# Turning two groups of sample outputs by VectorE and DMAs, later head sums, gates a head ahead, another last norm

## The chip, the cores and the metric

One core of a Trainium2 chip. The metric is the device time of one launch, in microseconds (us). The kernel before takes 2647.93 us, the median of 3 runs (2647.58 to 2648.16).

## What is computed

One inference step of a decoder with two layers on 320 tokens: a prompt of 256 new tokens and 8 samples of 8 new tokens each, width 2048, float32. Layer 0 mixes tokens by gated linear attention (GLA, 4 heads, with a carried state for each sample), layer 1 by a chunked spatial gate (SG); each layer has a squared-ReLU MLP of width 8192 behind it, and every block ends in a layer norm. The parts that the change touches, cut from the reference:

```python
def gla_chunked(q, k, v, log_a, s0):
    ...
        scores = jnp.where(causal, jnp.einsum('bhtk,bhsk->bhts', q_dec, k_inv), 0.0)
        o = (jnp.einsum('bhtk,bhkv->bhtv', q_dec, s)
             + jnp.einsum('bhts,bhsv->bhtv', scores, vi))
        s_new = (jnp.exp(b_last[..., 0, :])[..., None] * s
                 + jnp.einsum('bhsk,bhsv->bhkv', k_to_end, vi))
        return s_new, o

def gla_mixer(x, w_in, w_gate, b_gate, norm_g, w_out, s0):
    ...
    o, s_fin = gla_chunked(q, k, v, log_a, s0)
    o = o * lax.rsqrt(jnp.mean(jnp.square(o), axis=-1, keepdims=True) + HEAD_NORM_EPS) * norm_g
    o = o.reshape(bsz, t, GLA_VAL_DIM).astype(x.dtype) * jax.nn.silu(r)
    return o @ w_out, s_fin.astype(s0.dtype)

def layer_norm(x, g, b):
    ...
    return ((xf - mu) * lax.rsqrt(var + LN_EPS) * g + b).astype(x.dtype)
```

## The kernel before

**Weights and products.** Activations stand transposed: 128 features on the partitions, 320 tokens along the free axis (prompt 0 to 255, samples 256 to 319). Every weight matrix streams once from memory in units of 512 KB (128 x 1024 values). SyncE starts the load into `raw`; ScalarE casts it to fp32r, `wh` (L176); VectorE subtracts for the rest, `wl` (L177). A unit feeds 24 matmuls of 128x128 by 128x320, three for each product (`mm3`, L194 to L196: low weight by high activation, high by low, high by high). Four units are kept in a ring, so ScalarE can be at most four units ahead of TensorE. I call these matmuls "products" and count them from the start of GLA: w_in takes 96 units, products 1 to 2304; w_out begins with product 2305.

**GLA, head by head.** Each of four heads has 24 units of w_in: 8 for v (`project_v`), 8 for k and q (`project_kq`), 8 for r (`project_r`). Between units, a `Side` runs a step of a list. `Head.steps` is the list that starts with `project_r` of its head and goes on through the next head's `project_v`: scores (`sample_scores`, `prompt_scores`), outputs of the prompt (`prompt_o`), of the first sample group (`sample_first`, `sample_group`), splits of carried states into three bf16 parts (`split`), the new prompt state (`prompt_state`, which needs `split_kv`, the high and low parts `vk` of v and k), the second sample group, then `sums` (squares summed over the head's features and rsqrt, `rs`), `weigh` (gate and norm weight) and `finish` (times `rs`). For the last head the list has only the 8 units of `project_r` and 2 more.

A sample group's output comes out of TensorE with tokens on partitions and must be turned. `sample_out` copies it out of PSUM (`os`), has TensorE transpose it four times (L688), and copies and adds the three bf16 parts. `turn_out` instead turns 32x32 blocks on VectorE, adds the parts, and lets 16 small DMAs of GpSimd's queue put the blocks in place; `place_out` copies the result into `o_all`. Before, heads 0 to 2 use `turn_out` for one group and `sample_out` for the other; head 3 uses `sample_out` for both.

**w_out** starts with units whose activations are split ahead: `split_early` makes `early` (feature blocks 0 to 2) in storage that `vk` and others used, and `split_rest` makes `oh` and `ol` for the rest, head 3's last.

**The order.** A scheduler decides the order on each engine when the program is built, from the order of the code, buffers and dependences; on the chip an engine runs its list in that order. PSUM tiles `gl` (the small products), `vfm` (one buffer, used by `turn_out`, `sums` and the decayed keys) and others are handed out in the order of the code, so a step that stands later in the code waits for the tiles of those before it.

**The last norm.** `take` gathers sums and sums of squares of the 16 feature blocks (`A_`, `Q_`), TensorE adds over partitions with matrices of ones; the last two blocks' parts go in as float32 matmuls (L882, L883). Then 14 blocks are normed as TensorE (d plus the negated mean, split high and low, by an identity matrix), VectorE (`t`, L1267) and ScalarE (`z`, L1268), and two on GpSimd (L1258 to L1260); the outputs leave by SyncE's queue (L1270, L1272).

## Time and profile before

| what | before |
| --- | --- |
| median of 3 runs | 2647.93 us |
| the profiled execution | 2648.76 us |
| its span, first to last instruction | 2647.0 us |
| mean granted TensorE clock | 0.999 |
| MB moved by DMA | 525.61 (mean 199 GB/s) |

The 1.76 us between the execution's time and its span lie outside of what the profile sees. Engines: PE is TensorE, PEld its weight loads, DVE VectorE, ACT ScalarE, POOL GpSimd, SP SyncE. A row of a timeline has the start and the busy time, both in us, engine, line, operation, output and inputs, shapes, count, and in brackets the idle time before it and what ended that. Busy times of neighbours overlap a little, so the pitch from start to start says what one costs in a row. In the groups, the numbers behind the bar are busy us, mean ns of one, and idle time before.

### The profile page before, as it was taken

To read this page: it belongs to the slowest core of one execution; us is meant where nothing else is said; L and a number is where in the kernel's file an instruction comes from. 1 tells how busy PE (TensorE), PEld (TensorE's weight loads), DVE (VectorE), ACT (ScalarE), POOL (GpSimd) and SP (SyncE) were. 2 spreads that over 40 slices of the span, in tenths; PEclk is the share of its full clock that TensorE was granted. 3 is DMA by queue.
4 is the path that set the end of the run, shared out by engine and by line. 5 is a ranking of instruction groups with operands and counts; after the bars stand their busy time and mean duration, and the time that the engine had idled before them with its cause. 6 is when DMAs were issued, how large, how long until landed. Compare 5 with 4: busy or idle time off the path is not lost.

```text
span 2647.0 us, 47028 instructions
## 1 busy us (share of the span) xinstructions
PE 2638.0 (100%) x18347; PEld 2622.7 (99%) x18347; DVE 1898.2 (72%) x2799; ACT 1335.2 (50%) x2296; POOL 438.4 (17%) x743
## 2 busy tenths in 40 slices
PE   9999999999999999999999999999999999999998
PEld 9999999999999999999999999999999999999998
DVE  7787777886666667667578797787667667766656
ACT  6666665564454445444346544465445435444434
POOL 4354320001111111111000074001111111111000
PEclk9999999999999999999999999999999999999999
DMA  8667656457676767676545456447776767776642
GB/s 257 204 178 224 207 155 232 152 179 228 216 229 217 233 215 229 214 231 207 160 152 163 154 165 196 151 138 218 219 229 216 232 214 230 215 229 215 197 153 91
DMA packets 172799, 525.61 MB, mean 199 GB/s; under 512 B 34784, under 2 KB 43744, under 8 KB 172576
## 3 DMA queue, kind: packets, MB, share of 16 engines
q1 hardware_dynamic: 129504, 409.00, 49.0%
q0 software_dynamic: 42528, 112.94, 14.2%
q8 instruction: 144, 2.36, 0.4%
q14 instruction: 79, 0.65, 0.1%
q10 hardware_dynamic: 544, 0.66, 0.1%
HBM read 493.73 MB, written 22.55 MB: 195 GB/s over the span
## 4 chain that ended last, share of the span: by engine, by line
PE 99%; ACT 0%; DMA 0%; DVE 0%; issue 0%; ACTq 0%; DVEq 0%
PE mm L194 33%; PE mm L196 32%; PE mm L195 32%; PE gl L677 0%; PE gl L629 0%; PE gl L1195 0%; PE gl L611 0%; ACT z L1268 0%; PE gl L612 0%; PE gl L590 0%; DMA raw<-gla_w_in 0%; PE gl L596 0%; PE gl L348 0%; PE gl L347 0%; PE gl L688 0%; PE gl L667 0%
## 5 line engine op out<-in xcount | busy, mean ns | idle before, releaser
L177 DVE TENSOR_TENSOR wl<-raw,wh 128x1024 fp32r<-128x1024 f32 (+1 forms) x740 | 908.3, 1229 | 638.3 <-ACT wh L176 632.1
L176 ACT CAST wh<-raw 128x1024 fp32r<-128x1024 f32 (+1 forms) x740 | 771.6, 1044 | 1054.0 <-PE mm L196 924.7
L196 PE MATMUL mm<-yh,wh 128*128 128x320 f32 x2624 | 805.4, 307 | 0.0
L194 PE MATMUL mm<-yh,wl 128*128 128x320 f32 x2624 | 802.6, 308 | 0.0
L195 PE MATMUL mm<-yl,wh 128*128 128x320 f32 x2624 | 794.1, 303 | 0.0
L194 PE MATMUL mm<-hh,wl 128*128 128x320 f32 x2048 | 630.9, 308 | 0.0
L196 PE MATMUL mm<-hh,wh 128*128 128x320 f32 x2048 | 628.8, 307 | 0.0
L195 PE MATMUL mm<-hl,wh 128*128 128x320 f32 x2048 | 619.7, 303 | 0.0
L195 PEld LDWEIGHTS mm<-yl,wh 128*128 128x128 f32 x2624 | 492.6, 188 | 0.0
L194 PEld LDWEIGHTS mm<-yh,wl 128*128 128x128 f32 x2624 | 491.1, 188 | 0.0
L196 PEld LDWEIGHTS mm<-yh,wh 128*128 128x128 f32 x2624 | 490.8, 187 | 0.0
L194 PEld LDWEIGHTS mm<-hh,wl 128*128 128x128 f32 x2048 | 384.5, 188 | 0.0
L195 PEld LDWEIGHTS mm<-hl,wh 128*128 128x128 f32 x2048 | 384.5, 188 | 0.0
L196 PEld LDWEIGHTS mm<-hh,wh 128*128 128x128 f32 x2048 | 383.0, 187 | 0.0
L990 DVE SCALAR_TENSOR_TENSOR su<-vr,pace,su 128x512 f32<-128x512 f32 x512 | 362.9, 745 | 0.0
L961 POOL DMA_DIRECT2D vr<-v_dram x256 | 138.8, 542 | 1292.2 <-DVE su L990 1280.7
L194 PE MATMUL mm<-xh,wl 128*128 128x320 f32 x768 | 237.7, 311 | 0.3 <-DVE wl L177 0.3
L196 PE MATMUL mm<-xh,wh 128*128 128x320 f32 x768 | 237.1, 309 | 0.0
L195 PE MATMUL mm<-xl,wh 128*128 128x320 f32 x768 | 234.4, 305 | 0.0
L195 PEld LDWEIGHTS mm<-xl,wh 128*128 128x128 f32 x768 | 145.0, 189 | 2.0 <-issue 1.7
L194 PEld LDWEIGHTS mm<-xh,wl 128*128 128x128 f32 x768 | 144.8, 189 | 1.7 <-issue 0.8
L196 PEld LDWEIGHTS mm<-xh,wh 128*128 128x128 f32 x768 | 144.4, 188 | 1.3 <-issue 1.3
(294 smaller groups left out, 2542.8 us busy)
## 6 DMA issues: line engine op xcount, KB each, us to landing
raw<-mlp_w SPq DMA_DIRECT2D x512, 512.0 KB, 4.0
vr<-v_dram POOLq DMA_DIRECT2D x256, 256.0 KB, 4.2
raw<-gla_w_in SPq DMA_DIRECT2D x94, 512.0 KB, 4.1
raw<-sg_w_in SPq DMA_DIRECT2D x64, 512.0 KB, 3.6
st<-state SPq DMA_DIRECT2D x32, 512.0 KB, 5.0
raw<-gla_w_out SPq DMA_DIRECT2D x32, 512.0 KB, 4.4
su<-state POOLq DMA_DIRECT2D x32, 512.0 KB, 6.4
o_state_s<-su POOLq DMA_DIRECT2D x32, 512.0 KB, 4.1
```

Of the source, the lines that this page charges most:

```text
L176: nc.scalar.copy(hi[:, ks, :], raw[:, ks, :])
L177: nc.vector.tensor_sub(lo[:, ks, :], raw[:, ks, :], hi[:, ks, :].bitcast(F32))
L194: nc.tensor.matmul(ps, wl[:, kk, s], x_h, start=first, stop=False)
L195: nc.tensor.matmul(ps, wh[:, kk, s], x_l, start=False, stop=False)
L196: nc.tensor.matmul(ps, wh[:, kk, s], x_h, start=False, stop=last)
L961: nc.gpsimd.dma_start(vt[:, 0:4, :], v_dram[h, b * DS + t].rearrange("(a f) -> a f", f=P).partition_broadcast(P))
L990: nc.vector.scalar_tensor_tensor(st[:, kt, :], v, k[:, kt : kt + 1], st[:, kt, :], op0=ALU.mult, op1=ALU.add)
```

## The change

- `WARM`: ten warming matmuls of ones at the start where there were nine.
- Heads 0 to 2 turn both sample groups by `turn_out`; `place_out` is called twice. `sample_out` with its TensorE transposes is left to head 3.
- `sums`, `weigh` and `finish` of heads 0 to 2 move behind the next head's `begin_states` and first two splits.
- The gates of heads 1 to 3 (`gate_logits`, `gate_sums`, `gate_decays`) are made in the steps of the head before.
- `prompt_scores` is ordered behind `sample_scores` on TensorE.
- The last head's `finish` and `weigh` stay in their order.
- Last norm: `A_` and `Q_` take one block more, before their ones matmuls, which now take all in float32 (`stop=True` in `total` for the other norms). The mean goes in by one matmul with a matrix `two_r` whose rows 0 and 32 are ones and the rest zeros (row 32 of `nh` holds the low part) instead of two with the identity. GpSimd has three blocks (4, 9, 13) instead of two, with two operations each instead of three; they get d plus the mean from TensorE, which ScalarE copies out of PSUM. The first four outputs leave singly.

```diff
 NU = KT // UK
-WARM = 9
+WARM = 10
 LINE = 64
...
                     d0 = c * CH if c < 2 else W0 + (c - 2) * CH
-                    nc.tensor.matmul(pc[rows, d0 : d0 + CH], hd.kip[:, kt, c * CH : (c + 1) * CH],
+                    m = nc.tensor.matmul(pc[rows, d0 : d0 + CH], hd.kip[:, kt, c * CH : (c + 1) * CH],
                                      hd.qd[:, kt, c * CH : (c + 1) * CH], start=(kt == 0 and c < 2),
                                      stop=(kt == 1 and c == NCH - 1))
+                    behind(m, hd.scored)
                     if c < NCH - 1:
...
                 ki = hd.kis[:, kt].rearrange("p b c t -> p (b c t)")
-                nc.tensor.matmul(pc[:], ki, hd.qd[:, kt, TP:T], start=(kt == 0), stop=(kt == 1))
+                hd.scored = nc.tensor.matmul(pc[:], ki, hd.qd[:, kt, TP:T], start=(kt == 0), stop=(kt == 1))
             nc.vector.copy_predicated(scs[:], mask_s[:].rearrange("p a b -> p (a b)"), pc[:])
...
         def place_out(hd):
-            o_s = o_all[:, 4 * hd.h : 4 * hd.h + 4, TP : TP + 4 * DS].rearrange("p v (j t) -> p v j t", t=DS)
+            c0 = TP + 4 * DS * (hd.g - 1)
+            o_s = o_all[:, 4 * hd.h : 4 * hd.h + 4, c0 : c0 + 4 * DS].rearrange("p v (j t) -> p v j t", t=DS)
             nc.scalar.copy(o_s, hd.got.rearrange("p j v t -> p v j t"))
...
             last = hd.h == H - 1
+            n = None if last else hds[hd.h + 1]
+            gate = (lambda: None,) * 3 if last else (n.gate_logits, n.gate_sums, n.gate_decays)
             yield lambda: None
...
             yield split(5, lambda: (last and hd.sample_out(), hd.gather_k(3)))
-            yield split(6)
-            yield split(7, lambda: last or hd.turn_out())
-            yield hd.split_kv
+            yield split(6, gate[0])
+            yield split(7, lambda: (last or hd.turn_out(), gate[1]()))
+            yield lambda: (hd.split_kv(), gate[2]())
             yield lambda: (hd.prompt_state(0), hd.prompt_state(1), hd.sample_first(), hd.sample_group())
-            yield (lambda: (hd.place_out(), hd.sample_out())) if not last else lambda: (split_early(hd), hd.sample_out())
-            yield hd.sums
-            yield hd.weigh if hd.h < H - 1 else hd.finish
-            yield hd.finish if hd.h < H - 1 else hd.weigh
-            if hd.h < H - 1:
-                n = hds[hd.h + 1]
+            if last:
+                yield lambda: (split_early(hd), hd.sample_out())
+                yield hd.sums
+                yield hd.finish
+                yield hd.weigh
+            else:
+                yield lambda: (hd.place_out(), hd.turn_out())
                 yield n.begin_states
...
                 yield lambda: n.split(1)
+                yield lambda: (hd.place_out(), hd.sums())
+                yield hd.weigh
+                yield hd.finish
...
     for h, hd in enumerate(hds):
-        gates = [hd.gate_logits, hd.gate_sums, hd.gate_decays]
         states = [lambda n=n: hd.split(n) for n in range(4)]
...
             side = Side([lambda: None, lambda: load_x(1), lambda: None, lambda: load_x(2), lambda: load_gates(),
-                         lambda: load_x(3), low_gate, *gates], 4 * NU)
+                         lambda: load_x(3), low_gate, hd.gate_logits, hd.gate_sums, hd.gate_decays], 4 * NU)
             hd.project_v(side)
...
             hd.project_v(side)
-            hd.project_kq(Side([*gates, *states[2:]], 2 * NU))
+            hd.project_kq(Side(states[2:], 2 * NU))
         side = Side(hd.steps(), 2 * NU + (2 * NU if h < H - 1 else 2))
...
             nc.tensor.matmul(p[:], ones_r[:], lo[:], start=True, stop=False)
-            nc.tensor.matmul(p[:], ones_r[:], hi[:], start=False, stop=not self.last)
+            nc.tensor.matmul(p[:], ones_r[:], hi[:], start=False, stop=True)
             return p
...
                 nc.scalar.activation(Q_, d, AF.Square)
-            elif j < KT - 2 or not self.last:
+            elif j < KT - 1 or not self.last:
                 nc.vector.tensor_add(A_, A_, d)
                 nc.vector.tensor_add(Q_, Q_, s[:])
-            if j == KT - (3 if self.last else 1):
+            if j == KT - 1 and not self.last:
                 self.pA, self.pQ = self.total(A_), self.total(Q_)
-            if j >= KT - 2 and self.last:
-                nc.tensor.matmul(self.pA[:], ones[:], d, start=False, stop=(j == KT - 1))
-                nc.tensor.matmul(self.pQ[:], ones[:], s[:], start=False, stop=(j == KT - 1))
+            elif j == KT - 1:
+                self.pA, self.pQ = gltile(T), gltile(T)
+                for p, a, b in ((self.pA, A_, d), (self.pQ, Q_, s[:])):
+                    nc.tensor.matmul(p[:], ones[:], a, start=True, stop=False)
+                    nc.tensor.matmul(p[:], ones[:], b, start=False, stop=True)
             if self.raw is not None:
...
                 nc.scalar.activation(gh, d, AF.Identity, scale=g)
-                nc.vector.scalar_tensor_tensor(gl_, d, g, gh.bitcast(F32), op0=ALU.mult, op1=ALU.subtract)
+                i = nc.vector.scalar_tensor_tensor(gl_, d, g, gh.bitcast(F32), op0=ALU.mult, op1=ALU.subtract)
+                if self.last and j == KT - 2:
+                    self.rest = i
...
             else:
-                nc.vector.tensor_add(zj, zj, ps[:])
+                i = nc.vector.tensor_add(zj, zj, ps[:])
+                if last and j == KT - 1:
+                    behind(norm.rest, i)
             norm.add(j)
...
-    on_pool = (5, 9)
+    on_pool = (4, 9, 13)
     dh, dl = norm.raw
     ps = {}
-    t_pool = l2.tile([P, T], F32, tag="s", name="t_pool")
     ident_r = l2.tile([P, P], F32R, tag="s", name="ident_r")
...
-    on_pe = [j for j in range(KT) if j not in on_pool]
+    def add_mean(j):
+        nc.tensor.matmul(ps[j][:], two_r[:], nh[:], start=False, stop=True)
+
+    on_pe = [*on_pool, *(j for j in range(KT) if j not in on_pool)]
     nh = l2.tile([P, T], F32R, tag="r", name="nh")
-    nl = l2.tile([P, T], F32R, tag="f", name="nl")
+    two_r = l2.tile([P, P], F32R, tag="vt", name="two_r")
+    nc.gpsimd.memset(two_r[:].bitcast(F32), 0.0)
+    for r in (0, 32):
+        nc.gpsimd.memset(two_r[r : r + 1].bitcast(F32), 1.0)
...
         nc.scalar.copy(nh[:], norm.nd[:])
-        nc.vector.tensor_sub(nl[:], norm.nd[:], nh[:].bitcast(F32))
+        nc.vector.tensor_sub(nh[32:33], norm.nd[32:33], nh[32:33].bitcast(F32))
...
     oT = A["o_yT"].rearrange("(k p) t -> p k t", p=P)
-    m_pool = l2.tile([P, T], F32, tag="vt", name="m_pool")
-    nc.gpsimd.tensor_mul(m_pool[:], norm.nd[:], norm.rstd[:])
+    for j in on_pool:
+        add_mean(j)
+        nc.scalar.copy(z[:, j, :], ps[j][:])
+    scaled = None
     for j in range(KT):
...
         if j in on_pool:
-            nc.gpsimd.tensor_mul(t_pool[:], y, norm.rstd[:])
-            nc.gpsimd.tensor_add(t_pool[:], t_pool[:], m_pool[:])
-            nc.gpsimd.tensor_scalar(y, t_pool[:], g, b, op0=ALU.mult, op1=ALU.add)
+            i = nc.gpsimd.tensor_mul(y, y, norm.rstd[:])
+            if scaled is not None:
+                behind(i, scaled)
+            scaled = nc.gpsimd.tensor_scalar(y, y, g, b, op0=ALU.mult, op1=ALU.add)
         else:
...
             t = l2.tile([P, T], F32, tag="t", name=nm("t"), bufs=3)
-            nc.tensor.matmul(ps[j][:], ident_r[:], nl[:], start=False, stop=False)
-            nc.tensor.matmul(ps[j][:], ident_r[:], nh[:], start=False, stop=True)
+            add_mean(j)
             nc.vector.scalar_tensor_tensor(t[:], ps[j][:], g, norm.rstd[:], op0=ALU.mult, op1=ALU.mult)
             nc.scalar.activation(y, t[:], AF.Identity, bias=b)
-        if j < 2:
+        if j < 4:
             nc.sync.dma_start(oT[:, j, :], z[:, j, :])
```

Where it moves instructions, at the places of which the prediction speaks. The rows are those of an engine's list, in order; names are tiles of the program (`mm` products, `gl` small PSUM tiles, `sp` split states, with a number that tells instances apart).

TensorE before, around head 3's `prompt_state` (L629): weight products of w_in stand ahead of it, and 48 of them behind.

```order
L194 MATMUL mm_4610<-xh_95,wl_4648 128x320
L195 MATMUL mm_4610<-xl_96,wh_4647 128x320
L196 MATMUL mm_4610<-xh_95,wh_4647 128x320
L629 MATMUL gl_4677<-vk_4641,ktp_3969 128x512 x2
L629 MATMUL gl_4677<-va_3970,vk_4641 128x512 x2
L629 MATMUL gl_4677<-vk_4641 128x512 x2
L629 MATMUL gl_4685<-vk_4641,ktp_3969 128x512 x2
L629 MATMUL gl_4685<-va_3970,vk_4641 128x512 x2
L629 MATMUL gl_4685<-vk_4641 128x512 x2
L667 MATMUL gl_4694<-va_3970,scst 128x512
```

TensorE in the changed kernel, from the end of the first sample group of head 3 (L678; the last products of w_in stand ahead of all its rows) to `prompt_state` (now L630):

```order
L678 MATMUL gl_4515<-sp_4187,qm 32x512
L689 MATMUL gl_4588<-ident,os_4586 128x128 x4
L630 MATMUL gl_4717<-vk_4681,ktp_4051 128x512 x2
L630 MATMUL gl_4717<-va_4052,vk_4681 128x512 x2
L630 MATMUL gl_4717<-vk_4681 128x512 x2
L630 MATMUL gl_4725<-vk_4681,ktp_4051 128x512 x2
L630 MATMUL gl_4725<-va_4052,vk_4681 128x512 x2
L630 MATMUL gl_4725<-vk_4681 128x512 x2
L668 MATMUL gl_4734<-va_4052,scst 128x512
```

`prompt_state` moved from behind product 2256 to behind product 2304, the last of w_in, and the transposes of `os` (L689) stand directly ahead of it.

TensorE in the changed kernel, a little later: a row of the second sample group (L678) ahead of the first products of w_out, whose activations are `early` (before, these stood directly behind the last products of w_in):

```order
L678 MATMUL gl_4734<-sp_4605,qm 32x512
L194 MATMUL mm_4862<-early_4790,wl_4870 128x320
L194 MATMUL mm_4863<-early_4790,wl_4870 128x320
L194 MATMUL mm_4864<-early_4790,wl_4904 128x320
L194 MATMUL mm_4865<-early_4790,wl_4904 128x320
L195 MATMUL mm_4862<-early_4790,wh_4869 128x320
L196 MATMUL mm_4862<-early_4790,wh_4869 128x320
```

So no product stands between the end of w_in and that place.

ScalarE before, from the cast for `vk` (L404) to the copy `os` (L685); `sr`, the gate of the last products of w_in, comes 22 rows later:

```order
L404 CAST vk_4641<-va_3970 128x1024
L613 COPY o_all_97<-gl_4456 128x2x256
L615 ACTIVATE sq_4462<-gl_4456 128x512
L406 CAST vk_4641<-ktp_3969 128x512
L613 COPY o_all_97<-gl_4465 128x2x256
L615 ACTIVATE sq_4471<-gl_4465 128x512
L657 CAST sp_4509<-st_3964 128x1024
L657 CAST sp_4560<-st_4205 128x1024
L657 CAST sp_4565<-st_4242 128x1024
L685 COPY os_4546<-gl_4475 128x512
```

ScalarE in the changed kernel, from `sr`, which reads the products up to 2304, to the copy `os` (now L686):

```order
L564 ACTIVATE sr_4858<-mm_4650 128x320
L774 CAST oh_4860<-o_all_97 128x320 x5
L176 CAST wh_4975<-raw_4974 128x1024
L774 CAST oh_4860<-o_all_97 128x320 x7
L406 CAST vk_4681<-ktp_4051 128x512
L404 CAST vk_4681<-va_4052 128x1024
L614 COPY o_all_97<-gl_4505 128x2x256
L616 ACTIVATE sq_4511<-gl_4505 128x512
L658 CAST sp_4549<-st_3929 128x1024
L658 CAST sp_4600<-st_4155 128x1024
L658 CAST sp_4605<-st_4192 128x1024
L686 COPY os_4586<-gl_4515 128x512
```

The casts for `vk`, the prompt's outputs (L614, L616), the state casts (L658) and `os` moved from before the last `sr` to behind it and behind the casts `oh` of w_out.

## Prediction

> **What bounds the kernel now.** I read the page first: its busy times, its chain, its costliest groups.
>
> ```profile
> PE 2638.0 (100%) x18347; PEld 2622.7 (99%) x18347; DVE 1898.2 (72%) x2799; ACT 1335.2 (50%) x2296; POOL 438.4 (17%) x743
> PE 99%; ACT 0%; DMA 0%; DVE 0%; issue 0%; ACTq 0%; DVEq 0%
> L176 ACT CAST wh<-raw 128x1024 fp32r<-128x1024 f32 (+1 forms) x740 | 771.6, 1044 | 1054.0 <-PE mm L196 924.7
> ```
>
> TensorE (PE) works 2638.0 of 2647.0 us and makes up 99% of the chain; ScalarE (ACT), which splits the weights, stands 924.7 us waiting for PE to give a weight buffer back. Then the waits of PE, all there are:
>
> ```profile
> PE gl L185 <- DVE ones L143: 1.1, 1, 1.1
> PE mm L194 <- DVE wl L177: 0.3, 1, 0.3
> ```
>
> PE waits 1.4 us in the whole program, both times in the first 6 us. So an edit counts only if it changes PE's work, the ends of the span, or if it makes PE wait where it does not now. Saved time on ACT, VectorE (DVE) and GpSimd (POOL) is worth nothing by itself.
>
> All sums below are against the profiled execution (2648.76 us, span 2647.0). The median shown is 0.83 lower, and I take that off at the end.
>
> **The warming matmuls, the transposes, the gates.** The start of PE's timeline (start, busy):
>
> ```profile
> 1.12 4.21 PE L185 MATMUL gl<-ones 128*128 128x128 f32 x18 [1.12 <-DVE ones L143]
> 5.59 0.87 PE L194 MATMUL mm<-xh,wl 128*128 128x320 f32 x2 [0.27 <-DVE wl L177]
> 10.00 0.47 PE L196 MATMUL mm<-xh,wh 128*128 128x320 f32 x1
> 10.27 0.42 PE L194 MATMUL mm<-xh,wl 128*128 128x320 f32 x1
> 12.71 0.31 PE L196 MATMUL mm<-xh,wh 128*128 128x320 f32 x1
> 12.85 0.31 PE L194 MATMUL mm<-xh,wl 128*128 128x320 f32 x1
> ```
>
> Nine warming matmuls are 18 records in 4.21 us; a tenth is 0.47 us more and falls mostly into the 0.27 us in which PE waits for `wl`. Bounds: +0.2 (it pushes the first product) and -1.7 (matmuls start every 0.27 us until 10.27 and every 0.14 after 12.7, so half rate ending 3.4 us sooner would give 1.7). I take 0, as the gap of 0.27 is the nearest row.
>
> Heads 0 to 2 lose the four PE transposes of the second sample group (12 in all). One set in the chain:
>
> ```profile
> 121.73 0.44 PE gl L688 x4
> ```
>
> Three sets: **-1.3 us**. What replaces them (stream transposes and adds on DVE, 48 more DMAs issued by POOL, three more table loads on ACT) runs beside the weight products of the next head, with four weight units of 24 matmuls x 0.145 = 3.5 us prepared ahead. POOL, busy 17%, has room. I cost it at nothing; were that cover gone, each microsecond beyond some 14 would show.
>
> **The last norm.** Its tail:
>
> ```profile
> 2631.80 0.48 DVE L1247 TENSOR_TENSOR nl<-nd,nh 128x320 fp32r<-128x320 f32 x1
> 2633.85 6.51 DVE L1267 SCALAR_TENSOR_TENSOR t<-mm,vec,rstd 128x320 f32<-128x320 f32 x14
> 2634.43 6.52 ACT L1268 ACTIVATE z<-t,vec 128x320 f32<-128x320 f32 x14 [2.29 <-DVE t L1267]
> 2634.71 0.87 POOL L1258 TENSOR_TENSOR t_pool<-z,rstd 128x320 f32<-128x320 f32 x1
> 2636.65 0.61 POOL L1260 TENSOR_SCALAR z<-t_pool,vec 128x320 f32<-128x320 f32 x1
> ```
>
> One of 14 steps goes to POOL: 6.51 / 14 = -0.47 us on the DVE-ACT chain. Four matmuls of the sums go ahead of it: 4 x 0.145 = -0.58. The three PSUM copies that POOL now needs (about 0.45 each, as `z`) fit into ACT's 2.29 us of idle time. POOL does 3 x (0.87 + 0.61) = 4.4 us plus gaps from 2633.9, and ends near 2638.8, before the last `z` at 2640.9. **-1.05 us**; bounds 0 (POOL or the copies late) and -1.5.
>
> **The end of head 3: a new wait.** Here work moves, and nothing is saved. The sums of head 2 now stand behind head 3's `begin_states` and first splits; PSUM tiles `gl` are handed out in that order, so head 3's scores stand behind those sums. Counted over the PE rows of both orders: head 3's scores stood behind weight product 2136 and stand now behind 2255; `prompt_state` (L629, now L630) stood behind 2256 and now behind all 2304 products of w_in. The product that starts w_out needs `early`, whose storage is that of `kqx`/`vk`, free only after L630; it is PE's next product and cannot be passed. So from T0, the end of product 2304, PE has only head 3's own small work, and that hangs on ACT. ACT's order after T0 (its rows are shown with the change): `sr` (it waits for product 2304), 12 `oh`, one `wh`, L406, L404, L614, L616, three L658, then L686 `os`. On `os` waits L689, and behind L689 on PE stand L630, L668, L678 and all of w_out. The same instructions before:
>
> ```profile
> 365.55 1.04 ACT L404 CAST vk<-va 128x1024 fp32r<-128x1024 f32 x1
> 369.15 0.62 ACT L406 CAST vk<-ktp 128x512 fp32r<-128x512 f32 x1 [1.30 <-DMA ktp<-blk]
> 369.68 0.58 ACT L613 COPY o_all<-gl 128x512 f32<-128x512 f32 x1
> 370.15 0.60 ACT L615 ACTIVATE sq<-gl 128x512 f32<-128x512 f32 x1
> 370.64 2.94 ACT L657 CAST sp<-st 128x1024 bf16<-128x1024 f32 x3
> 373.48 0.59 ACT L685 COPY os<-gl 128x512 f32<-128x512 f32 x1
> 373.95 1.06 ACT L176 CAST wh<-raw 128x1024 fp32r<-128x1024 f32 x1
> 395.95 0.44 ACT L564 ACTIVATE sr<-mm 128x320 f32<-128x320 f32 x1 [0.66 <-PE mm L196]
> 396.29 1.53 ACT L766 CAST oh<-o_all 128x320 fp32r<-128x320 f32 x4
> ```
>
> They ran in the order that the program lists, so I add starts to starts: sr 0.34, 12 oh x 0.36 = 4.3, wh 0.95, L406 0.53, L404 0.95, L614 0.47, L616 0.49, three L658 2.84, os 0.6: **`os` is there at T0 + 11.5**. PE's side and the last links:
>
> ```profile
> 369.38 1.48 PE L677 MATMUL gl<-sp,qm 128*32 128x512 bf16 x24
> 383.20 0.62 PE L629 MATMUL gl<-vk,ktp 128*128 128x512 f32 x2
> 385.98 0.40 PE L667 MATMUL gl<-va,scst 128*128 128x512 f32 x1
> 386.31 1.04 PE L677 MATMUL gl<-sp,qm 128*32 128x512 bf16 x14
> 371.79 3.49 DVE L658 TENSOR_TENSOR st<-st,sp 128x1024 f32<-128x1024 f32 x3
> 382.09 1.22 DVE L658 TENSOR_TENSOR st<-st,sp 128x1024 f32<-128x1024 f32 x1
> 384.88 1.22 DVE L660 TENSOR_TENSOR sp<-st,sp 128x1024 bf16<-128x1024 f32 x1
> 385.24 0.58 ACT L631 COPY S<-gl 128x512 f32<-128x512 f32 x1
> 386.67 0.82 ACT L766 CAST early<-o_all 128x320 fp32r<-128x320 f32 x2
> 387.16 0.89 DVE L767 TENSOR_TENSOR early<-o_all,early 128x320 fp32r<-128x320 f32 x2
> ```
>
> L689 ends at T0 + 12.0, L630 (385.98 - 383.20 = 2.8) at 14.8, L668 with 14 L678 (1.3) at 16.1. DVE meanwhile: the three L659 from about 9.2 to 12.5 (3.4), two L661 to 14.8, L694, a third L661 and L694 to 16.3, the fourth L659 to 17.5, then `early` low: 18.0. ACT, through three L660 and an L658 to 15.4, two S copies and `early` high, is done before that. PE can do four products (0.6) without `early` low, so w_out is under way as from T0 + 17.4. PE's own work in the stretch is 0.6 (L612, L613) + 1.8 (L668 with 24 L678) + 0.44 + 2.8 + 1.3 = 6.9. **PE idles 17.4 - 6.9 = 10.5 us**, some 9 of them in one piece ahead of L689. Bounds: 9.2 (DVE and `early` hidden, 16.1 - 6.9) and 13 (busy times in place of pitches, and semaphores).
>
> After that piece PE restarts. The only start from rest in this trace is the program's: half pitch from 1.12 to 10.27, 9.15 us. At half pitch the 4.5 us from L689 to the last of the 14 L678 take 9.0, w_out starts at T0 + 20.6 instead of 17.4: +3.2. Without that, 0. I take **+1.6**, between: the first stretch was made of short matmuls with a gap, this one is dense.
>
> By the Trainium skill's "TensorE: Matmul & The Clock Gate", Part 1 (The HAM clock gate), an idle window of about 3.4 us puts PE back to half clock until a busy one has passed, whose place is free-running. An estimate from that page alone would be +0.9 to +2.5 here. This trace shows the half rate at the start (the 0.27 pitch until 10.27) but no re-throttling, since PE never rests later. The rule speaks against this change: rest costs more than its own length.
>
> **Sum.** 2648.76 - 1.3 - 1.05 + 10.5 + 1.6 = 2658.5; less 0.83: **2658 us**.
>
> **The rivals.**
> - *The same wait, PE at full rate behind it.* 2656.1. For it: no rest of PE inside the trace shows a drop. 0.25.
> - *No wait that costs: not slower.* Place: `os` in front of L689. PE's own work covers T0 to about T0 + 2.4; if ACT delivers `os` by then, the price is 0 and the time 2645.6; below an idle time of some 7 us in all it stays within 0.2%. That needs ACT's 11.5 us to shrink to some 8 or less. For it: four weight units lie ready, and PE waited nowhere in GLA before. Against it: `sr` cannot start before T0, and what stands behind it is ACT's own busy time. 0.13, partial cases included (about 2650).
> - *A second wait, for head 3's share of w_out.* The sums of head 3 stand now behind product 2416 (before 2346), the first product that reads head 3's low part behind 2508 (before 2461): the cover was 115 products x 0.145 = 16.7 us and is now 92 x 0.145 = 13.3, against a chain (`ny`, `nw`, `rs`, four L581, L575, `oh`, `ol`, with weight splits between) of some 11 to 13. If it does not hold, +5: 2663. 0.12.
> - *The warming matmul ends half rate a window sooner,* with no wait: 2643.9, still within 0.2%. 0.02; *gains I do not see*: 0.03.
>
> **How the numbers follow.** The forecast itself has 0.45; with its rival at full rate, 0.7 for 2655 to 2661. The range leaves out the case without a wait, and takes in the second wait and the bounds: 2649 to 2664. 0.2% (5.3 us) is about what a measurement of this kernel can tell from no change. Slower by more than that, above 2653.2: 0.45 + 0.25 + 0.12 = 0.82. Within: 0.14. Faster: 0.04.
>
> **What would show it.** In the changed profile: PE's waits list a wait of L689 for `os` of 8 to 10 us near 390, and one for `early` of 1 to 3; the page's PE row falls to about 99.3% of the span; `sr`, `oh`, L404, L658 and `os` follow each other on ACT without idle time. The first products of w_out at a pitch of 0.27 would show the slow restart, L629's six pairs taking 5.6 us too. PE stays unbroken elsewhere; L688 has 8 records instead of 20; the tail from the last weight product to the end is about 1 us shorter. If L689 has no wait, my reading of the order is wrong, and with it the sign.

## The result and the profile after

| | before | after |
| --- | --- | --- |
| median of 5 runs (lowest to highest), us | 2647.72 (2647.45 to 2648.16) | 2668.71 (2667.35 to 2671.53) |
| span of the profiled execution, us | 2647.0 | 2667.0 |
| ratio, 95% interval | | 1.0081 (1.0071 to 1.0092) |

The change costs 21 us. The sign was forecast; the size was not: 2658 with a range up to 2664. From the page of the profile after the change: the busy times, the chain and the weight casts.

```profile
PE 2638.0 (99%) x18325; PEld 2620.5 (98%) x18325; DVE 1895.7 (71%) x2804; ACT 1338.6 (50%) x2296; POOL 461.7 (17%) x793
PE 94%; DMA 2%; ACT 2%; DVE 2%; issue 1%; SPq 0%; ACTq 0%; DVEq 0%
L176 ACT CAST wh<-raw 128x1024 fp32r<-128x1024 f32 (+1 forms) x740 | 771.4, 1044 | 1045.8 <-PE mm L196 923.0
```

PE is busy as long as before, 2638.0 us, in a span 20 us longer: so on balance all of the loss is time in which PE waits. The chain that ended last runs outside of PE for 6% of the span. PE's waits after (us in total, times, longest):

```profile
PE gl L689 <- ACT os L686: 8.7, 1, 8.7
PE mm L194 <- DVE wl L177: 7.7, 3, 4.8
PE mm L194 <- DVE vst L511: 1.5, 1, 1.5
PE gl L630 <- issue: 1.4, 1, 1.4
PE gl L185 <- DVE ones L143: 1.1, 1, 1.1
PE mm L194 <- DVE nw L223: 0.6, 1, 0.6
PE mm L195 <- DVE early L775: 0.4, 1, 0.4
PE mm L195 <- DVE xl L267: 0.2, 1, 0.2
```

The wait of L689 for `os` is the one forecast for the end of w_in. The timeline of PE there (T0, the end of product 2304, is 396.9):

```profile
408.62 1.09 PE L689 MATMUL gl<-ident,os 128*128 128x128 f32 x4 [8.66 <-ACT os L686]
409.36 1.20 PE L630 MATMUL gl<-vk,ktp 128*128 128x512 f32 x2
410.36 1.05 PE L630 MATMUL gl<-va,vk 128*128 128x512 f32 x2
411.22 0.80 PE L630 MATMUL gl<-vk 128*128 128x512 f32 x2
411.85 0.63 PE L630 MATMUL gl<-vk,ktp 128*128 128x512 f32 x2
...
414.53 0.85 PE L194 MATMUL mm<-early,wl 128*128 128x320 f32 x4
415.74 0.41 PE L195 MATMUL mm<-early,wh 128*128 128x320 f32 x1 [0.35 <-DVE early L775]
```

`os` comes at T0 + 11.7, and w_out is under way, past `early`, at T0 + 18.9. The other waits, 11.2 us (7.7 + 1.5 + 1.4 + 0.6), were not forecast. 10.6 of them lie between 236 and 348 us, in the products of heads 2 and 3, where nothing was to wait; the 0.6 with `nw` lie in w_out, at 438.62. The two longest, on PE, among head 3's products of k and q:

```profile
340.25 0.63 PE L194 MATMUL mm<-xh,wl 128*128 128x320 f32 x1 [4.82 <-DVE wl L177]
...
343.34 0.31 PE L196 MATMUL mm<-xh,wh 128*128 128x320 f32 x1
...
347.93 0.42 PE L194 MATMUL mm<-xh,wl 128*128 128x320 f32 x1 [2.52 <-DVE wl L177]
```

and ScalarE just ahead of them:

```profile
332.59 1.05 ACT L658 CAST sp<-st 128x1024 bf16<-128x1024 f32 x1 [5.32 <-DMA st<-state]
335.62 1.04 ACT L658 CAST sp<-st 128x1024 bf16<-128x1024 f32 x1 [1.99 <-DMA st<-state]
...
337.52 1.04 ACT L176 CAST wh<-raw 128x1024 fp32r<-128x1024 f32 x1
```

ScalarE waits 7.3 us for carried states, and the next weight cast stands behind them in its list. The four weight units that I counted as cover do not help when the engine that fills them stands still. Why the states are late is what the experiments are about.

### The profile page after: what moved, and what is told of

Its sections match the earlier page's. It is cut to its first block, busy times and chain, and to the rows that moved or that the text cites. A ratio compares the mean times of both kernels' runs of the same rounds, so it can differ in the third digit from the quotient of the medians.

```text
span 2667.0 us, 47071 instructions
## 1 busy us (share of the span) xinstructions
PE 2638.0 (99%) x18325; PEld 2620.5 (98%) x18325; DVE 1895.7 (71%) x2804; ACT 1338.6 (50%) x2296; POOL 461.7 (17%) x793
## 4 chain that ended last, share of the span: by engine, by line
PE 94%; DMA 2%; ACT 2%; DVE 2%; issue 1%; SPq 0%; ACTq 0%; DVEq 0%
PE mm L194 31%; PE mm L196 31%; PE mm L195 30%; DMA st<-state 1%; DVE wl L177 1%; ACT sp L658 0%; DMA raw<-gla_w_in 0%; ACT wh L176 0%; SPq L372 0%; DMA raw<-gla_w_out 0%; DVE sp L661 0%; PE gl L1208 0%; DVE st L659 0%; PE gl L630 0%; ACT z L1288 0%
## 5 line engine op out<-in xcount | busy, mean ns | idle before, releaser
L194 PEld LDWEIGHTS mm<-xh,wl 128*128 128x128 f32 x768 | 144.5, 188 | 11.2 <-DVE wl L177 8.9
```

The costliest lines, as they stand in the source:

```text
L194: nc.tensor.matmul(ps, wl[:, kk, s], x_h, start=first, stop=False)
```

## The experiments

Each kernel is the change with one edit, unless the text says otherwise. Times are medians; the kernel before was run beside each, at 2647.6 to 2648.3 us.

**Are the small gains what I took them for?** Two kernels from the kernel before: `norm_only` takes the new norm and `WARM`, `warm_only` this line alone.

```diff
-WARM = 9
+WARM = 10
```

> Only the new last norm and the tenth warming matmul; the GLA part as before. The prediction's terms: 0 for the warming matmul (bounds +0.2 and -1.7) and -1.05 us for the norm (bounds 0 and -1.5): 1.05 us under the kernel before, and all of the loss of the change gone. If instead the new norm or the start brings a wait, this run is not below the kernel before.

> The kernel before with ten warming matmuls instead of nine, and nothing else. The prediction took 0, with bounds +0.2 and -1.7. In the profile of before the half rate ends at 10.3 us, in all five profiles with ten it ends at 6.4 to 7.0. If the tenth matmul does that: -1.2 to -1.7, 2646.1 to 2646.6. If the place of a free-running window decides by chance: no difference beyond 0.5 us, and the half rate may end at either place.

Measured: 2647.16 us, ratio 0.9997 (0.9987 to 1.0006), and 2647.29 us, 0.9997 (0.9988 to 1.0007). Neither can be told from no change. The new norm adds nothing visible to the warming matmul.

**Where do the waits between 236 and 348 us come from?** (The expectations call them the waits in heads 1 to 3.) My first two theories were the gates made a head ahead, and the place of the sums in the code. `gates_own` makes the gates in their own head again:

```diff
-            gate = (lambda: None,) * 3 if last else (n.gate_logits, n.gate_sums, n.gate_decays)
+            gate = (lambda: None,) * 3
...
+        gates = [hd.gate_logits, hd.gate_sums, hd.gate_decays]
...
-            hd.project_kq(Side(states[2:], 2 * NU))
+            hd.project_kq(Side([*gates, *states[2:]], 2 * NU))
```

> The whole change, but every head makes its gates in its own steps, as before. Theory A (the prediction's: the sums stand behind the next head's first splits, the gl tiles go in that order, and that makes head 3 late): the sums stand where the change put them, so some 10 us of waits stay, 2658 to 2668. Theory B (the gates ahead fill ScalarE and VectorE in the stretch where the states are split and the second group is turned, and only both together make the heads late): in the order of this kernel head 3's prompt_state stands behind product 2256 again (2304 in the change, 2256 before), so the waits go, and -1.3 - 1.05 us remain: about 2645.5.

`sums_first` puts the sums ahead of the next head's states in the code:

```diff
-                yield n.begin_states
-                yield lambda: n.split(0)
-                yield lambda: n.split(1)
                 yield lambda: (hd.place_out(), hd.sums())
                 yield hd.weigh
                 yield hd.finish
+                yield n.begin_states
+                yield lambda: n.split(0)
+                yield lambda: n.split(1)
```

> The whole change, but sums, weigh and finish of heads 0 to 2 stand in the code ahead of the next head's begin_states and first two splits. Theory A: head 3's scores come earlier, the wait at the end of w_in goes, about 2646 to 2655. Theory B: the place in the code decides nothing (the small products stand behind the same weight products as in the change, 2255 for head 3's scores and 2304 for its prompt_state): 2665 to 2672, with L689 waiting some 9 us.

`one_turned` leaves the second group of heads 0 to 2 to TensorE's transposes, and keeps all the rest of the change:

```diff
-                yield lambda: (hd.place_out(), hd.turn_out())
+                yield lambda: (hd.place_out(), hd.sample_out())
...
-                yield lambda: (hd.place_out(), hd.sums())
+                yield hd.sums
```

> The whole change, but the second sample group of heads 0 to 2 goes out by TensorE transposes as before; gates ahead, sums late, new norm. Theory A: sums late, so the waits stay, 2658 to 2668. Theory B: prompt_state of head 3 stands behind product 2256 again, the waits go; the 12 transposes are back (+1.3), so -1.05 us remain: about 2646.8. If the gates ahead alone were the cause, this run would be as slow as the change.

Measured: `gates_own` 2693.33 us (1.0171, 1.0156 to 1.0186), far worse than the change and above both numbers that I had. Its waits of PE begin with

```profile
PE mm L194 <- DVE qd L490: 35.8, 3, 13.4
```

so the gates made ahead are not the cost; beside the second turn they keep it down. `sums_first` 2668.13 us, like the change: on TensorE the sums stand where they stood, and the place in the code is not the cause. `one_turned` 2646.66 us, 0.9995 (0.9985 to 1.0005): PE waits neither between 236 and 348 us, but for 0.2 us ahead of head 2's own transposes, nor at the end of w_in. So the loss hangs on the second turn.

**Is it the queue?** `ot_sync` and `ot_act` issue the second group's 16 DMAs on SyncE's and on ScalarE's queue. The edit for SyncE (`[...]` stands for what stays):

```diff
-                    nc.gpsimd.dma_start(hd.got[...], sent[...])
+                    (nc.sync if hd.g else nc.gpsimd).dma_start(hd.got[...], sent[...])
```

> The whole change, but the 16 small DMAs of the second group's turning go out on SyncE's queue and not on GpSimd's, where they stood among the gathers of v of the next head. Theory C (the turned second group comes back late because of that queue; so the sums are late, and all that takes a gl tile behind them: the next head's scores, states, and head 3's prompt_state): the order has the sums of head 2 behind product 1986 instead of 2255 and head 3's prompt_state behind 2256 instead of 2304; the waits go, and -1.3 (transposes), -1.6 (half rate ends sooner, as in all profiles with ten warming matmuls) and 0 to -1 (norm) remain: 2645 to 2646.5. Rival D (turning by DMA is late on any queue): L689 waits some 9 us, 2660 to 2670. Rival E (SyncE's queue feeds the weights, and 16 issues of 0.6 us keep them back): DVE's wl late, waits of PE on wl, 2650 to 2660.

> The same, with these 16 DMAs on ScalarE's queue. Theory C: head 3's prompt_state behind product 2256 again, no wait at the end of w_in: 2645 to 2648. Rival D: 2660 to 2670. A rival of its own: ScalarE issues them itself, in front of the weight casts; 16 x 0.6 us would be some 10 us without a cast for each of three heads, which four units of weights (13.9 us) just cover, or do not: up to 2655.

Measured: 2660.72 us (1.0049, 1.0034 to 1.0064) and 2666.94 us (1.0071, 1.0054 to 1.0088). Neither has a wait of L689 any more, and both have others, so neither comes to the 2645 to 2648 of theory C. On SyncE's queue, in `ot_sync`:

```profile
132.89 11.10 SPq L710 DMA_DIRECT2D ot<-ot  x16
```

Weight loads stand behind these 11.1 us, and PE waits 10.0 us for `wl` in all. In `ot_act` they take 13.4 us of ScalarE's queue. PE waits 13.5 us in all for `vst`, to which VectorE adds the low part (L511) behind ScalarE's cast (L510), and ahead of that cast ScalarE stands 38.4 us in all for these DMAs. On each queue that I tried, the 16 DMAs cost time.

**How is it spread over the heads?** `turned_01` and `turned_0` turn twice by DMAs only in heads 0 and 1, and only in head 0. The edit of `turned_0` (`turned_01` has `hd.h == H - 2` in place of `hd.h >= 1`; both also leave out `place_out` ahead of those heads' `sums`):

```diff
-                yield lambda: (hd.place_out(), hd.turn_out())
+                yield lambda: (hd.place_out(), hd.sample_out() if hd.h >= 1 else hd.turn_out())
```

> The whole change, but head 2's second group goes out by TensorE transposes, as before; heads 0 and 1 are turned twice. It tells the wait at the end of w_in (head 3 late because of head 2's sums) from the waits between 236 and 348 us (heads 1 and 2). Theory C: the order has head 3's scores behind product 2136 again, its prompt_state behind 2298; the 8.7 us of L689 shrink to 0 to 4, while the waits around 240 and 324 (3.2 us) stay: 2649 to 2656. If the waits at 340 and 348 (7.3 us), in front of which ScalarE stands for state loads of head 3, stay too, the upper end.

> The change, with the second sample group of heads 1 and 2 turned by TensorE's transposes, so that only head 0 turns twice by DMAs. In the list of TensorE, sums stand behind 993, 1439 and 1967 (change: 993, 1646, 2255; before 815, 1335, 1935), head 2's scores behind 1584 again and head 3's prompt_state behind 2260. Theory (the delay adds up from head to head): only head 1's waits stay (0.4 for wl near 237, 1.5 for vst near 242), none at 340 and 348 and none of L689: 2646.5 to 2649.5 us. Rival (each head that turns twice costs the same by itself): 20.8 / 3 = 7 us, or (20.8 - 7 of the end of w_in) / 2 = 7 us: 2652 to 2655.

Measured: 2661.53 us (1.0050, 1.0035 to 1.0065), above what I expected, and 2659.55 us (1.0043, 1.0029 to 1.0057). Without head 2's second turn the wait of L689 is gone; 7.2 us go with it. But head 0 alone costs 11.7 us, against both of my numbers: its delay is not made up in head 1, and behind head 2, which turns once, PE still waits 4.3 us (at 339.54, among head 3's products). So it does not add up head by head as I had put it.

**The result or the queue?** By then my theory was that the DMAs' result comes late, the sums with it, and whatever takes a PSUM tile behind the sums. In `no_dma` the second group is placed straight from VectorE's tile, with no DMAs; `dma_idle` adds 16 DMAs into a buffer in memory that nobody reads, `idle_8` and `idle_4` have `range(2)` and `range(1)` there; `late_sums` has no DMAs, and late sums by the edit shown further below for `one_turned_late`. In these five, the blocks of that group stand in the wrong places. The edit of `dma_idle` (`no_dma` is without its three lines on `idle`):

```diff
+            if hd.g:
+                hd.got = ot[:, 0, :].rearrange("p (j v t) -> p j v t", j=4, v=4)
+                for i in range(4):
+                    for j in range(4):
+                        nc.gpsimd.dma_start(A["idle"][32 * i : 32 * (i + 1), j], tb[32 * j : 32 * (j + 1), i, :, 0, :])
+            else:
                 for i in range(4):
                     for j in range(4):
                         nc.gpsimd.dma_start(hd.got[...], sent[...])
```

> The change, but the 16 small DMAs of the second sample group of heads 0 to 2 are left out: place_out copies straight from the tile that VectorE wrote (so the blocks of those sample outputs, and of what is computed from them, stand in the wrong places). VectorE's transposes and adds and ScalarE's copy stay. In the list of TensorE, sums then stand behind products 831, 1365 and 1941 (change: 993, 1646, 2255), head 3's scores behind 2136 again and its prompt_state behind 2256. Theory (the way through the DMAs is late, and what stands behind it drifts): the waits of L689, wl and vst go, PE waits under 3 us in all, 2645 to 2648 us. Rival (VectorE's and ScalarE's additional work, or the place of the sums in the code, is the cost): the waits in heads 1 to 3 stay, 2655 us or more.

> As no_dma (the second sample group of heads 0 to 2 is placed straight from VectorE's tile, in the wrong places), but GpSimd still issues 16 small DMAs for it, from the tile of the turned blocks to a scratch buffer in memory that nothing reads. So the queue has the work of the change, and nobody waits for a result. In the lists, sums stand early again (831, 1467, 2041; change 993, 1646, 2255), but GpSimd's list has the 16 DMAs among the gathers of the next head's v as in the change, and prompt_state of heads 1 to 3 stands behind 1304, 1920 and 2304 (change 1309, 1920, 2304; no_dma 1187, 1780, 2256). Theory Q (GpSimd's queue is the cost: the gathers of v come late behind the 16 DMAs): waits for wl or vst in heads 1 to 3 and of L689 come back, 2656 to 2670 us. Theory L (the late result and the late sums are the cost): waits under 3 us, 2645 to 2649 us.

> As no_dma, but sums, weigh and finish of heads 0 to 2 are moved into the first steps of the next head's project_r and ordered behind the last weight product made so far: TensorE has the sums behind 1034, 1610 and 2186 (change 993, 1646, 2255; no_dma 831, 1365, 1941), the next head's scores behind them at 1056, 1632 and 2186, prompt_state behind 1224, 1800 and 2256. GpSimd's list is that of no_dma. Theory Q (the queue is the cost, late sums are not): waits under 3 us, 2645 to 2649 us. Theory L (late sums push what stands behind them): waits in heads 1 to 3 of 5 us or more, 2652 us or more.

> As dma_idle, with 8 idle DMAs in GpSimd's queue in place of 16. In the lists prompt_state of heads 1 to 3 stands behind 1243, 1828 and 2298 (16 DMAs: 1304, 1920, 2304; none: 1187, 1780, 2256). Theory Q (the queue, by its length): between no_dma and dma_idle, waits of 2 to 12 us, 2649 to 2662 us; the wait of L689 goes or shrinks, as six products of w_in now stand behind prompt_state. Rival (it is not the length but that DMAs stand there at all, or a threshold): as dma_idle, 2666 or more, or as no_dma, under 2647.

> As dma_idle, with 4 idle DMAs in GpSimd's queue; prompt_state of heads 1 to 3 stands behind 1208, 1782 and 2256, within 21 products of the kernel without any. Theory Q: waits of under 4 us, 2645 to 2650 us. Rival (DMAs there at all): 2655 or more.

Measured, with the products of w_in behind which TensorE's list has head 0's sums and head 1's `prompt_state`, and the start of that `prompt_state` (first row of its matmuls, us) in the trace:

| kernel | DMAs in GpSimd's queue for the second group | sums | `prompt_state` | it starts at | time, us | ratio (95%) |
| --- | --- | --- | --- | --- | --- | --- |
| `no_dma` | 0 | 831 | 1187 | 202.20 | 2645.35 | 0.9991 (0.9982 to 1.0000) |
| `late_sums` | 0 | 1034 | 1224 | 207.52 | 2644.65 | 0.9989 (0.9980 to 0.9998) |
| `idle_4` | 4, unread | 831 | 1208 | 205.41 | 2644.39 | 0.9987 (0.9978 to 0.9997) |
| `idle_8` | 8, unread | 831 | 1243 | 210.19 | 2652.06 | 1.0018 (1.0009 to 1.0027) |
| `dma_idle` | 16, unread | 831 | 1304 | 219.02 | 2668.77 | 1.0083 (1.0066 to 1.0100) |
| the change | 16 | 993 | 1309 | 219.67 | 2668.71 | 1.0081 (1.0071 to 1.0092) |

PE's waits in `no_dma`, and those over 2 us in `dma_idle`:

```profile
PE gl L185 <- DVE ones L143: 1.1, 1, 1.1
PE mm L194 <- DVE wl L177: 0.3, 1, 0.3
```

```profile
PE mm L194 <- DVE wl L177: 8.8, 3, 3.9
PE gl L689 <- ACT os L686: 8.7, 1, 8.7
```

This decides what the loss hangs on. With DMAs that nobody reads, and sums earlier than the change's (831, 1467 and 2041), the whole loss is back, the wait of L689 too; with sums about as late as the change's (1034, 1610 and 2186; 993, 1646 and 2255) and no DMAs, there is none. My theory of the late result falls. The cost follows the number of DMAs given to GpSimd's queue, with room for some: 4 cost nothing, 8 some 7 us, 16 some 23 (each against `no_dma`).

What they displace is seen in POOL's timeline between head 0 and head 1, first `no_dma`, then the change:

```profile
159.27 1.13 POOL L372 DMA_DIRECT2D va<-blk  x2 [0.30 <-DMA va<-blk]
...
164.10 8.68 POOL L372 DMA_DIRECT2D ktp<-blk  x16 [1.94 <-DVE kqx L493]
```

```profile
135.89 2.49 POOL L710 DMA_DIRECT2D ot<-ot  x5
139.06 1.12 POOL L710 DMA_DIRECT2D ot<-ot  x2 [0.68 <-DMA va<-blk]
141.57 4.40 POOL L710 DMA_DIRECT2D ot<-ot  x9 [1.39 <-DMA va<-blk]
...
162.38 3.35 POOL L372 DMA_DIRECT2D va<-blk  x6 [0.32 <-DMA va<-blk]
...
173.94 8.68 POOL L372 DMA_DIRECT2D ktp<-blk  x16 [4.00 <-DVE blk L482]
```

In the change the 16 DMAs stand among the gathers of head 1's v (`va`); the last six of these take until 165.7, where `no_dma` is done with them at 160.4. The gathers of k (`ktp`) start at 173.9 instead of 164.1. But the queue is empty ahead of them, 4.0 us here, until VectorE has turned k's blocks (L482). In head 2 of the change, and in head 1 of `dma_idle`, where v's gathers are done at 159.1, it is empty for longer:

```profile
280.64 8.69 POOL L372 DMA_DIRECT2D ktp<-blk  x16 [14.23 <-DVE blk L482]
```

```profile
156.80 2.27 POOL L372 DMA_DIRECT2D va<-blk  x4 [0.96 <-DMA va<-blk]
...
170.83 5.46 POOL L372 DMA_DIRECT2D ktp<-blk  x10 [7.37 <-DVE blk L482]
```

`prompt_state` needs both gathers, and in the change ScalarE's cast of k for it runs 32 us behind the issue of the last one, in head 1 as in head 2:

```profile
214.84 0.60 ACT L406 CAST vk<-ktp 128x512 fp32r<-128x512 f32 x1
219.67 0.63 PE L630 MATMUL gl<-vk,ktp 128*128 128x512 f32 x2
```

Neither row has idle time ahead of it, so the engines did not stand there for the gathers: they came to these rows later. In TensorE's list `prompt_state` of head 1 has 122 products more ahead of it than in `no_dma`, 17.7 us at 0.145, and it starts 17.5 us later. So there the delay is that of the lists, which were fixed when the program was built with these DMAs in it, and time lost in the queue on the chip is not what the rows show.

The loads of the next head's states go on SyncE's queue where `prompt_state` stands: at 219.35 (before 201.65), in head 2 at 325.42 (before 300.28). There the queue shows

```profile
325.42 14.04 SPq L652 DMA_DIRECT2D st<-state  x4
340.23 0.34 SPq L170 DMA_DIRECT2D raw<-gla_w_in  x1
```

and of SyncE's waits (us in total, times, longest)

```profile
SPq L652 <- DVE sp L661: 23.6, 8, 12.2
```

The fourth of these loads holds the queue for those 12.2 us, until VectorE is done with an earlier state, and the weight loads stand behind it. ScalarE's waits for the states are those shown above, ahead of the weight casts. One row of the windows there (us of the stretch; busy us of PE, PEld, DVE, ACT, POOL; granted clock, DMA share, GB/s):

```profile
336.00:350.00 14.00, 7.22 (x38) 6.97 (x39) 13.30 (x21) 9.88 (x13) 5.86 (x11) 0.88 0.59 179
```

PE works half of it, VectorE nearly all of it: behind the wait it has weights and states to split at once.

**Is the half rate behind the wait its price?** `fill` puts 64 matmuls of ones where PE rests ahead of L689:

```diff
+            for _ in range(64 if hd.h == H - 1 and hd.g == 0 else 0):
+                behind(nc.tensor.matmul(pt[:, 0:P], ones[:], ones[:], start=True, stop=True), hd.grouped)
```

> The change, with 64 matmuls of ones (128x128 by 128x128, float32, on the result tile before the transposes overwrite it) put on TensorE between the first sample group of head 3 and the transposes of os, where TensorE rests 8.7 us. They need nothing but a free PSUM tile, so TensorE works in that rest. Theory (the rest brings half rate for some 2.9 us, over and above its length): L630's pitch behind it is 0.47 per pair in place of 0.6 to 1.0, w_out begins 1 to 1.5 us sooner after os, 2667.0 to 2668.0 us. Rival 1 (the half rate hides behind VectorE's low part of early): L630 at full pitch, but the first product of w_out waits for early longer, no change of the time. Rival 2 (the half rate has another cause than rest): the rows stay as in the change. The wait itself stays in all three (ScalarE's chain to os is untouched).

Measured: 2671.14 us (2668.05 to 2672.57). PE in `fill`:

```profile
397.23 14.56 PE L689 MATMUL gl<-ones 128*128 128x128 f32 x128
411.62 0.60 PE L691 MATMUL gl<-ident,os 128*128 128x128 f32 x4
411.98 0.71 PE L630 MATMUL gl<-vk,ktp 128*128 128x512 f32 x2
```

The matmuls took 14.4 us where 8.7 were free (`os` lay ready from 405.8), so the time says nothing. The rows behind do: all six pairs of L630 at a pitch of 0.46 to 0.55, where the change has 1.00, 0.86 and 0.63 for the first three. So it is the rest that brings the half rate.

**Is there something better than both?** `one_turned` again, and `one_turned_late`, the same with the late sums of `late_sums`, which computes all that the reference does (`product[0]` is the last weight product made so far):

```diff
-            nc.tensor.matmul(pr[:], ones_r[:], lo[:], start=True, stop=False)
+            behind(nc.tensor.matmul(pr[:], ones_r[:], lo[:], start=True, stop=False), product[0])
...
-                yield hd.sums
-                yield hd.weigh
-                yield hd.finish
...
+            yield hds[hd.h - 1].sums if hd.h else lambda: None
+            if hd.h:
+                yield hds[hd.h - 1].weigh
+                yield hds[hd.h - 1].finish
```

> The change, with the second group of heads 0 to 2 turned by TensorE's transposes, as in the run of the same kernel: is it below the kernel before by more than the measurement is uncertain? Theory: everything that is left of the change (new norm, tenth warming matmul, late sums, gates ahead) is worth -0.5 to -1.5 us: 2646.2 to 2647.3, ratio 0.9995 to 0.9998, not told apart from 1. Rival: the new norm's shorter tail and the sooner full rate add up to -2.5: 2645.2, ratio 0.999.

> one_turned (the change with TensorE's transposes for the second group of heads 0 to 2) with the late sums of late_sums: behind 1034, 1610 and 2186 (one_turned: 815, 1342, 1938), prompt_state behind 1224, 1800 and 2256. It computes all that the reference does. By the two runs of one_turned (2646.7) and the step from no_dma to late_sums (-0.7): 2645.5 to 2647 us. If late sums are a gain of their own (TensorE then finds what it needs ready), 2645.5 or less and the interval leaves 1 out; if late_sums' step was scatter, 2646.7, not told apart from the kernel before.

Measured: 2646.76 us, 0.9995 (0.9986 to 1.0004), and 2646.88 us, 0.9997 (0.9988 to 1.0006). Both are better than the change by 22 us, neither can be told from the kernel before. Late sums bring nothing of their own.

## Why the forecast was right in sign and wrong in size

- **"I cost it at nothing"** (what replaces the transposes in heads 0 to 2) is the step that failed. Besides the wait at the end of w_in there were 11.2 us of waits, 10.6 of them in heads 2 and 3, and 1.4 us of half rate behind the one of 4.8 us (eleven matmuls from 340.25 to 343.34, 3.09 us; at full rate 0.25 + 10 x 0.147 = 1.7). My reason was "POOL, busy 17%, has room", with four weight units ahead as cover. `dma_idle` against `no_dma` shows that 16 small DMAs more for each of three heads in GpSimd's queue cost 23.4 us though nobody reads them, and 4 nothing. Both of my reasons look past this: the share of the span says nothing of what stands around the DMAs, and the cover bounds a late result, where what came late was other work.
- **The wait at the end of w_in** was right in place and size: `os` at T0 + 11.7 (forecast 11.5), 9.1 us of waits for `os` and `early` (10.5), w_out past `early` at T0 + 18.9 (17.4 + 1.6 = 19.0). Its cause, as I put it, was wrong. I had the late sums of head 2 push head 3's small products through the order of the PSUM tiles. `late_sums` has them nearly as late (behind 2186 for 2255) and no wait; `dma_idle` has them early, and L689 waits 8.7 us. The rows of the order were right, my reading of what had moved them was not: the DMAs had.
- **The slow restart**, +1.6: L689 and the first three pairs of L630 took 3.23 us from start to start (408.62 to 411.85), in `fill` 1.83: +1.4. `fill` shows that the rest brings it. The rule of the Trainium skill's "TensorE: Matmul & The Clock Gate", Part 1 (The HAM clock gate), that about 3.4 us of idling bring the half rate back, agrees with the rests of 4.8 and 8.7 us, which bring it, and that of 2.5 us (347.93), which doesn't. In other kernels here rests of 1.8 to 3.1 us, below, bring it too; there the measurement decides.
- **The transposes**, -1.3: `no_dma` against `one_turned` in the same set of runs is 2645.35 - 2646.76 = -1.4. Right.
- **The warming matmul**, 0 within -1.7 and +0.2: the mechanism that I gave 0.02 took place. The start of PE after:

```profile
1.13 4.52 PE L185 MATMUL gl<-ones 128*128 128x128 f32 x20 [1.13 <-DVE ones L143]
...
6.39 0.42 PE L195 MATMUL mm<-xl,wh 128*128 128x320 f32 x1 [0.25 <-DVE xl L267]
6.64 0.31 PE L196 MATMUL mm<-xh,wh 128*128 128x320 f32 x1
```

  Half rate is over by 6.6 instead of 10.3. In the profile that is some 14 matmuls at 0.147 instead of 0.267, -1.7; in the times of `warm_only` -1.0, with an interval that holds 0.
- **The last norm**, -1.05: from the last addition to `z` (2628.92 before, 2650.37 after) to the end of the last `z` it was 12.0 and is 11.9. The 13 steps save their 0.46 (6.05 for 6.51), but the first of them starts 5.28 us behind that addition instead of 4.93:

```profile
2650.37 0.49 DVE L1040 TENSOR_TENSOR z<-z,mm 128x320 f32<-128x320 f32 x1 [0.16 <-PE mm L196]
...
2655.65 6.05 DVE L1287 SCALAR_TENSOR_TENSOR t<-mm,vec,rstd 128x320 f32<-128x320 f32 x13
```

  The four matmuls that I took off were not on that path.
- **The rival of a second wait** for head 3's share of w_out did not come: PE does not wait behind product 2508, where that share begins. The 0.6 us that the profile puts to head 3's `nw` lie 60 products earlier, at the start of a weight unit.

The sum with what was measured: 2645.6 (my case without a wait) + 9.1 + 1.4 + 11.2 + 1.4 = 2668.7, against 2668.71. That it fits so closely is partly luck: the two small gains came out other than forecast, and nearly cancel.

**Open.** Shown is that the number of DMAs given to GpSimd's queue makes the loss. How is in part read from the traces. VectorE's transposes of k (L482), ahead of which the queue stands empty, have no idle time ahead of them and stand later in VectorE's list. Whether the chip would lose anything with the lists of `no_dma` and the DMAs of the change was not tried, so the share of the queue on the chip and that of the lists stay open. Nor was it tried whether the scheduler put these rows later for the queue or for a buffer: in `dma_idle` the DMAs also hold the tile `tb` until they have read it. The last links, from the late `prompt_state` over the state loads to the weight casts, are read from the trace; `no_dma` too has ScalarE waiting for states, 13.2 us in all, but where weights lie ready.

## What to carry to other kernels

Before small DMAs are given to a queue with "room", look at what stands behind them at that place, and not at the queue's share of the span; then compare the lists of the other engines with and without them. To tell a late result from the DMAs themselves, issue the same DMAs and let nobody read them. Where an order shifts, find out which edit shifts it before giving the shift a cause: the same rows had two explanations, and only runs could tell them apart.

## What the hardware showed unexpectedly

- Half rate also comes after short rests, and some time after work has begun again. In `turned_0` it follows a rest of 3.14 us, 1.1 us after PE has started again:

```profile
240.03 0.41 PE L194 MATMUL mm<-xh,wl 128*128 128x320 f32 x1 [3.14 <-DVE wl L177]
...
241.41 0.47 PE L196 MATMUL mm<-xh,wh 128*128 128x320 f32 x1
...
244.60 0.31 PE L196 MATMUL mm<-xh,wh 128*128 128x320 f32 x1
```

  It lasts 3.4 us (241.2 to 244.6) in the midst of dense work, and this rest cost 1.5 us more than its length. The shortest such rest is one of 1.76 us, in `sums_first`:

```profile
338.21 0.42 PE L194 MATMUL mm<-xh,wl 128*128 128x320 f32 x1 [1.76 <-DVE wl L177]
339.71 0.47 PE L194 MATMUL mm<-xh,wl 128*128 128x320 f32 x1
342.91 0.32 PE L194 MATMUL mm<-xh,wl 128*128 128x320 f32 x1
```

  Rests of 2.0 (`idle_8`, 238.92) and 2.4 us (`turned_01`, 349.56) bring it as well, while one of 2.5 in the change (347.93) and one of 2.4 in `fill` (345.27) do not. So the length of a rest alone does not decide it.
- With ten warming matmuls half rate was over by about 7 us in all eighteen profiles; the one profile with nine has it until 10.3.
- A DMA of 32 partitions takes the issuing queue about 0.5 us on GpSimd (4.40 us for 9 above), 0.6 to 0.7 on SyncE (10.02 to 11.10 for 16) and 0.7 to 0.9 on ScalarE (11.06 for 16, 13.42 for 15), waits between them included.
